# A four-layer mixer trunk: the convolution layers' output projection taken block by block, and the first layer's norm of block 1 beside its first tile

## The chip, the cores and the metric

The kernel runs on one core of a Trainium2 chip. The metric is device time in microseconds of one execution; the profile comes from one further execution that the hardware profiler recorded.

## What is computed

One step of a hybrid trunk over 128 context and 1024 latent tokens of width 1024, four layers. Layers 0 and 3 are widened Conformer convolutions, layer 1 is gated neighbourhood attention, layer 2 a gated bidirectional scan. Each layer is a modulated RMSNorm, a mixer and a gated residual; a final RMSNorm follows. The convolution mixer is the part that matters here:

```python
def modulated_norm(x, cond, ada_w, ada_b, norm_w):
    mod = jax.nn.silu(cond) @ ada_w + ada_b
    shift, scale, gate = jnp.split(mod[:, None, :], 3, axis=-1)
    h = rms_norm(x, norm_w) * (1 + scale) + shift
    return h, gate

def conformer_conv_mixer(h, w_in, b_in, w_dw, b_dw, ln_w, ln_b, w_out, b_out):
    v, g, z = jnp.split(h @ w_in + b_in, 3, axis=-1)
    u = v * jax.nn.sigmoid(g)
    u = depthwise_conv(u, w_dw, b_dw)
    u = jax.nn.silu(layer_norm(u, ln_w, ln_b))
    return (u * jax.nn.silu(z)) @ w_out + b_out
```

## The kernel before

The 1152 tokens are three blocks (b0, b1, b2) of 384 columns; the width is eight tiles of 128 partitions. Every product with a weight is made in three passes of split numbers: `unit` (L466) runs, for each of eight k, `wh·hh` (L471), `wh·hl` (L472) and `wl·hh` (L473), 24 matmuls for one output tile of one block. Weight tiles come by DMA from SP's queue into `raw`, and `wsplit` (L432, L433) makes `wh` on ACT and `wl` on `w_eng`, which is GpSimd (POOL) but in layer 2; `wh` and `wl` have two buffers each, and one weight ahead is split when a weight is taken.

The order of the work is the order in which the program issues it, engine by engine. After each unit `tick` runs some of the work that stands in lists: up to four `steps` (the convolution's taps among them) and three advances (`GENS_A_UNIT`) of the first generator in `gens`, which holds norms. A norm is such a generator. `rstd` and `rstd_row` issue the sum over partitions, `st_ps` (L303 or L314; the latter after ACT has copied `row`, L312), and the twelve small VectorE operations `nr_a`, `nr_y`, `nr_z` of `rsqrt` (L323 to L331), called the chain below; `spread` then yields LAG = 4 times and issues `dg` (L340, VectorE), the matmul `rs_ps` (L344) that spreads the row, and `rstd` (L346, ACT). After that the norm issues per k `nt` (L360, VectorE), `hh` (L363, ACT) and `hl` (L364, VectorE), or in the convolution's LayerNorm `conv_norm` (L705): `mu` (L716, ACT), c − mu (L720, VectorE for even k, POOL for odd), its square (L722, ACT), the sum `var` (L723, PE), then the chain, then the scaling (L731, VectorE), silu (L733, ACT), the product with the gate path z, which is read back from DRAM (L734, VectorE), `gh` (L735, ACT) and `gl` (L736, POOL).

`start` runs 16 conditioning tiles (`ada_tile`, L244, L253) and norm 0 of block 0 among them, then block 1's, then hands block 2's to `gens`. `conv_layer` (L603) then loops over eight tiles of the width: the units of g and v of all three blocks, and the depthwise convolution `dwconv` of the tile, whose taps run on VectorE (L775), ACT and POOL beside the next tile's units. The last tile's taps of blocks 1 and 2 (`rest`), the LayerNorms and the units of z's last tile fill what follows. `out_proj` (L576) then projects: the first weights (m = 0, 1) for b0 and b1, m = 2 to 7 each for b0 and b1, and then all eight again for b2. `out_unit` adds the residual (`xm`, read from DRAM; L557, L566) and the sum of squares (L292 to L296), and `next_norm` hands the next layer's norm of a finished block to `gens`. In layer 3 a transposed final norm follows each unit instead (L1515, L1517).

Of the kernel before, what the change touches and what calls it, by code (L numbers as in the profile page):

```python
# [9 lines left out]
F32 = mybir.dt.float32  # L10
# [9 lines left out]
P = 128  # L20
D = 1024
KT = D // P
# [49 lines left out]
TAIL = {0: TAIL0, 3: TAIL3}  # L72


REST = 4
# [5 lines left out]
VAR_MM = 2  # L81

# [78 lines left out]
def run(steps):  # L161
    for s in steps:
        s()
        yield
# [10 lines left out]
class Kern:  # L175
    def __init__(self, ctx, tc, A, O, depth):
        self.tc, self.nc, self.A, self.O = tc, tc.nc, A, O
        nc = self.nc
        self.const = ctx.enter_context(tc.tile_pool(name="const", bufs=1))
        self.blkp = ctx.enter_context(tc.tile_pool(name="blk", bufs=9))  # L180
        self.wraw = ctx.enter_context(tc.tile_pool(name="wraw", bufs=3))
        self.wsp = ctx.enter_context(tc.tile_pool(name="wsp", bufs=2))
        self.work = ctx.enter_context(tc.tile_pool(name="work", bufs=2))
        self.dram = ctx.enter_context(tc.tile_pool(name="dram", bufs=1, space=DRAM))
        self.mmp = ctx.enter_context(tc.tile_pool(name="mm", bufs=3, space=PSUM))
        self.xs = [A["x"]] + [self.dram.tile([P, KT, T], F32, name=f"xs{i}") for i in range(1, DEPTH)]
        self.pend, self.steps, self.trickle, self.gens, self.slow = [], [], [], [], []
        self.raws, self.split, self.wi = {}, {}, 0
        self.w_eng = nc.gpsimd
        self.h = [None] * NB  # L190
        self.ada_end = lambda: None
        self.depth = depth
        self.specs = self.weight_specs()
# [177 lines left out]
    def weight_specs(self):  # L371
# [5 lines left out]
        for l in range(self.depth):  # L377
# [27 lines left out]
                        for i in SSD_ADA[b][m]:  # L405
                            ada(l + 1, i)
            if kind != 2:
                out += [(w[m], P) for g in range(2) for m in range(KT)]
        return out

    def wload(self, i, pool=None):
# [12 lines left out]
    def wsplit(self, i):  # L424
        if i < len(self.specs) and i not in self.split:
            nc = self.nc
            self.wload(i)
            width, raw = self.specs[i][1], self.raws.pop(i)
            wh = self.wsp.tile([P, KT, P], F32R, name="wh", tag="wh")
            wl = self.wsp.tile([P, KT, P], F32R, name="wl", tag="wl")  # L430
            s = raw[:, :, :width]
            nc.scalar.copy(out=wh[:, :, :width], in_=s)  # L432
            self.w_eng.tensor_tensor(out=wl[:, :, :width], in0=s, in1=wh[:, :, :width].bitcast(F32),  # L433
                                     op=ALU.subtract)
            self.split[i] = wh, wl

# [43 lines left out]
    def tick(self):  # L480
        for _ in range(STEPS_A_UNIT):
            if not self.steps:
                break
            self.steps.pop(0)()
        for _ in range(GENS_A_UNIT):
            self.advance()
        if self.slow and next(self.slow[0], StopIteration) is StopIteration:
            self.slow.pop(0)
        for _ in range(2):
            if self.trickle:  # L490
                self.trickle.pop(0)()
        due, self.pend = self.pend, []
        for e in due:
            e[0] -= 1
        for e in due:
            if e[0] <= 0:
                e[1]()
        self.pend = [e for e in due if e[0] > 0] + self.pend
# [77 lines left out]
    def out_proj(self, l, g, bias=None, order=None):  # L576
        nc = self.nc
        with self.tc.tile_pool(name="xm", bufs=2, reuse_waits="tile") as pool:
            self.out_begin(l, bias, pool)
            for grp in ((0, 1), (2,)):  # L580
                x0, x1 = (grp[0] * BW, (grp[-1] + 1) * BW) if order is None else (0, T)
                for ms in [(0, 1)] + [(m,) for m in range(2, KT)]:
                    w, xm = {}, {}
                    for m in ms:
                        w[m] = self.wtake()
                        xm[m] = pool.tile([P, x1 - x0], F32, name="xm", tag="xm", bufs=2)
# [16 lines left out]

    def conv_layer(self, l, j, order):
        nc, tc, h = self.nc, self.tc, self.h
        with tc.tile_pool(name="cp", bufs=1, space=PSUM, reuse_waits="tile") as cp, ExitStack() as stack:
            cw = stack.enter_context(tc.tile_pool(name="cw", bufs=2, reuse_waits="tile"))
            close = stack.close
# [75 lines left out]
            due, self.pend = self.pend, []  # L684
            for e in due:
                e[1]()
            self.lz = cw
            rest = run(chain(*rest))
            lns[0] = also(lns[0], rest, REST)
            z, nz = chain(*[z_tile(m) for m in TAIL[l][1]]), NB * len(TAIL[l][1])  # L690
            interleave(part(z, TAIL[l][2]), TAIL[l][2], part(lns[0], 9), 9)
            for _ in rest:
                pass
            lns[0] = also(lns[0], part(lns[1], 9))
            interleave(part(lns[0], TAIL[l][3]), TAIL[l][3], z, nz - TAIL[l][2])
            self.flush()
            close()
            with tc.tile_pool(name="lz", bufs=3, reuse_waits="tile") as self.lz:
                for _ in lns[0]:
                    pass  # L700
                self.gens += lns[1:]
                self.out_proj(l, g, bias=("conv_b_out", j * KT), order=order)

    def conv_norm(self, cp, b, j, c, s1, sums, zd, g):

        nc = self.nc
        if b == VAR_MM:
            self.var = cp.tile([P, 3 * 512], F32, name="var", tag="ca", bufs=1)
        if b < 2:
            sums(KT - 1, (b,))  # L710
        else:
# [6 lines left out]
        var = self.var[:, 512 * b:512 * b + BW] if b >= VAR_MM else self.mm("var")[:, :BW]  # L718
# [6 lines left out]
        r = yield from self.rstd_row(var, D, LN_EPS)  # L725
        gh, gl = self.blk(f"gh{b}", F32R), self.blk(f"gl{b}", F32R)
        for k in range(KT):
            z = self.lz.tile([P, BW], F32, name="zk", tag="zk", bufs=3)
# [4 lines left out]
            nc.scalar.activation(out=ck, in_=ck, func=AF.Silu, bias=self.v("conv_ln_b", j * KT + k))  # L733
            nc.vector.tensor_tensor(out=ck, in0=ck, in1=z, op=ALU.mult)  # L734
            nc.scalar.copy(out=gh[:, k, :], in_=ck)  # L735
            nc.gpsimd.tensor_tensor(out=gl[:, k, :], in0=ck, in1=gh[:, k, :].bitcast(F32), op=ALU.subtract)  # L736
            yield
        g[b] = gh, gl

# [797 lines left out]
    def start(self, pool):  # L1537
# [31 lines left out]
        for k in range(KT):  # L1569
# [2 lines left out]
                if RAW0 + 2 * k + i < 2 * KT:  # L1572
                    load(RAW0 + 2 * k + i)
            if k == NORM_0:
                steps(0, 1 + LAG + k)
            elif k > NORM_0:
                steps(0, 1)
            if k == TURN_1:
# [3 lines left out]
        self.ada_end()  # L1582
        steps(0, 9)
        self.wsplit(2 * KT + 1)
        steps(1, 1 + LAG + 9)
        self.x_sums(2)
        self.gens.append(self.norm(0, 2, self.xb[2], self.acc[2], self.h))

# [92 lines left out]
```

## Time and profile before

| | |
|---|---|
| median of 3 executions | 2966.41 us (2965.76 to 2966.68) |
| profiled execution | 2963.28 us, its span 2961.5 us |
| mean granted PE clock | 0.975 |
| PE busy | 2789.2 us (94%), 17561 matmuls |
| VectorE (DVE), ACT, POOL busy | 69%, 42%, 45% |
| layer 0's convolution loop | to about 400 us |
| layer 0's projection ends | 582.3 us |
| layer 3's projection ends | 2948.7 us |

How to read it: the profiled execution took 1.8 us more than its span, and stands 3.1 us under the median. A matmul of 384 columns starts about 0.17 us after the one before it at full clock, and its record is longer than that, since matmuls overlap. fp32 matmuls (`var`, `st_ps`, `rs_ps`) leave two records each. Idle time in front of an instruction stands behind it in brackets, with what ended it.

### The profile page before, as it was taken

The page shows a single profiled execution, that of the slowest core. Times are in us where ns is not written, and L with a number is a line of the kernel's source. Part 1 is how long each engine was busy: PE and PEld are TensorE (multiplying, and loading weights), DVE is VectorE, ACT ScalarE, POOL GpSimd, SP SyncE. Part 2 cuts the span into 40 slices and gives each one's busy share as a digit, 9 for nine tenths or more (in the row PEclk, how much of TensorE's full clock was granted, in tenths as well). Part 3 has the DMA queues.
Part 4 walks back from the last instruction along what each step waited for, and adds up shares of the span by engine and source line. Part 5 has one row for each costly group of instructions (what it writes and reads, how often), then busy time and mean ns, then how long its engine had stood idle before and what let it go on. Part 6 is the DMA issues. An engine that isn't in the chain of part 4 may idle for free. (4 is left out here: it accounts for less than half of the span.)

```text
span 2961.5 us, 45878 instructions
## 1 busy us (share of the span) xinstructions
PE 2789.2 (94%) x17561; PEld 2527.8 (85%) x17561; DVE 2047.6 (69%) x3319; ACT 1249.9 (42%) x2188; POOL 1347.5 (45%) x800
## 2 busy tenths in 40 slices
PE   5999988899999999999999999998899999999888
PEld 4999967889999998888999998877667889999678
DVE  5899886553554445537887778977986565999963
ACT  4455455443333333444443333222323444555553
POOL 4688766611001110244114443634644346888755
PEclk8999999999999999999999999999999999999989
DMA  5232324632222233335235559876886752111134
GB/s 220 65 121 97 102 82 146 226 105 83 73 84 85 88 91 90 120 116 188 87 105 173 167 177 325 304 219 210 253 288 223 254 179 93 54 59 58 63 119 141
DMA packets 231547, 424.45 MB, mean 143 GB/s; under 512 B 19552, under 2 KB 149408, under 8 KB 231328
## 3 DMA queue, kind: packets, MB, share of 16 engines
q1 hardware_dynamic: 229280, 417.50, 43.9%
q10 hardware_dynamic: 2048, 4.02, 0.4%
q8 instruction: 139, 2.28, 0.3%
q14 instruction: 80, 0.66, 0.1%
HBM read 331.83 MB, written 79.66 MB: 139 GB/s over the span
## 5 line engine op out<-in xcount | busy, mean ns | idle before, releaser
L433 POOL TENSOR_TENSOR wl<-raw,wh 128x1024 fp32r<-128x1024 f32 x169 | 407.8, 2414 | 960.0 <-ACT wh L432 916.7
L775 DVE SCALAR_TENSOR_TENSOR ca<-u,vec,ca 128x1167 f32<-128x1167 f32 (+4 forms) x420 | 481.5, 1146 | 11.3
L768 POOL TENSOR_TENSOR pa<-pa,pt 128x1167 f32<-128x1167 f32 (+4 forms) x189 | 399.6, 2116 | 78.1 <-ACT pa L763 37.0
L432 ACT CAST wh<-raw 128x1024 fp32r<-128x1024 f32 (+1 forms) x239 | 249.4, 1044 | 404.9 <-PE op L472 89.6
L471 PE MATMUL in_ps<-hh,wh 128*128 128x384 f32 x768 | 268.4, 352 | 3.9 <-DVE nt L866 2.7
L472 PE MATMUL in_ps<-hl,wh 128*128 128x384 f32 x768 | 262.5, 342 | 0.7 <-DVE hl L364 0.7
L473 PE MATMUL in_ps<-hh,wl 128*128 128x384 f32 x768 | 262.0, 341 | 0.0
L767 ACT ACTIVATE pt<-u,vec 128x1167 f32<-128x1167 f32 (+4 forms) x189 | 194.1, 1039 | 126.0 <-POOL pa L768 124.6
L471 PE MATMUL op<-gh,wh 128*128 128x384 f32 x576 | 201.8, 351 | 14.7 <-ACT gh L735 8.8
L473 PE MATMUL op<-gh,wl 128*128 128x384 f32 x576 | 199.8, 348 | 12.5 <-POOL wl L433 12.5
L1289 DVE SCALAR_TENSOR_TENSOR sca<-ub,vec,sca 128x1155 f32<-128x1155 f32 x144 | 205.0, 1423 | 3.5
L471 PE MATMUL x_ps<-hh,wh 128*128 128x384 f32 x576 | 203.2, 353 | 1.4 <-ACT ub L1240 0.7
L472 PE MATMUL op<-gl,wh 128*128 128x384 f32 x576 | 201.4, 350 | 0.8 <-POOL gl L736 0.8
L473 PE MATMUL x_ps<-hh,wl 128*128 128x384 f32 x576 | 196.0, 341 | 0.0
L472 PE MATMUL x_ps<-hl,wh 128*128 128x384 f32 x576 | 195.9, 340 | 0.0
L471 PEld LDWEIGHTS in_ps<-hh,wh 128*128 128x128 f32 x768 | 145.4, 189 | 13.6 <-issue 7.0
L296 POOL TENSOR_TENSOR ssq<-ssq,sq 128x384 f32<-128x384 f32 x105 | 110.5, 1054 | 86.4 <-ACT sq L295 85.2
L472 PEld LDWEIGHTS in_ps<-hl,wh 128*128 128x128 f32 x768 | 145.6, 190 | 3.2 <-DVE hl L364 1.5
L473 PEld LDWEIGHTS in_ps<-hh,wl 128*128 128x128 f32 x768 | 145.5, 190 | 3.1 <-issue 2.4
L471 PE MATMUL op<-sgh,wh 128*128 128x384 f32 x384 | 135.1, 352 | 6.5 <-DVE xm L566 2.5
L473 PE MATMUL sz_ps<-hh,wl 128*128 128x384 f32 x384 | 139.3, 363 | 0.0
L473 PE MATMUL op<-sgh,wl 128*128 128x384 f32 x384 | 133.5, 348 | 4.9 <-POOL wl L433 4.3
(281 smaller groups left out, 7605.0 us busy)
## 6 DMA issues: line engine op xcount, KB each, us to landing
raw<-in_ada_w SPq DMA_DIRECT2D x96, 512.0 KB, 4.6
rw<-ssd_rows SPq DMA_DIRECT2D x72, 512.0 KB, 5.7
raw<-in_ssd_w_in SPq DMA_DIRECT2D x62, 512.0 KB, 4.3
raw<-in_conv_w_in SPq DMA_DIRECT2D x48, 512.0 KB, 3.5
raw<-in_ssd_w_out SPq DMA_DIRECT2D x48, 512.0 KB, 4.4
raw<-in_conv_w_out SPq DMA_DIRECT2D x32, 512.0 KB, 3.6
raw<-in_na_w_in SPq DMA_DIRECT2D x32, 512.0 KB, 3.5
ssd_xtok<-xtk SPq DMA_DIRECT2D x20, 576.0 KB, 3.5
```

Of the source, the lines that this page charges most:

```text
L296: nc.gpsimd.tensor_tensor(out=acc, in0=acc, in1=sq, op=ALU.add)
L432: nc.scalar.copy(out=wh[:, :, :width], in_=s)
L433: self.w_eng.tensor_tensor(out=wl[:, :, :width], in0=s, in1=wh[:, :, :width].bitcast(F32), op=ALU.subtract)
L471: nc.tensor.matmul(out, lhsT=wh[:, k, :width], rhs=hh[:, k, :], start=f, stop=False)
L472: nc.tensor.matmul(out, lhsT=wh[:, k, :width], rhs=hl[:, k, :], start=False, stop=False)
L473: nc.tensor.matmul(out, lhsT=wl[:, k, :width], rhs=hh[:, k, :], start=False, stop=l)
L767: nc.scalar.activation(out=pt, in_=u_t, func=AF.Copy, scale=wt(t))
L768: nc.gpsimd.tensor_tensor(out=p, in0=p, in1=pt, op=ALU.add)
L775: nc.vector.scalar_tensor_tensor(out=c, in0=u_t, scalar=wt(t), in1=c, op0=ALU.mult, op1=ALU.add)
L1289: nc.vector.scalar_tensor_tensor(out=ca, in0=u[:, t:t + SCLEN], scalar=wt(t), in1=ca, op0=ALU.mult, op1=ALU.add)
```

## The change

Three things are done.

First, at the start, `rs_ps` of block 0 is issued after two more conditioning tiles, and block 1's norm is put into `gens`, so that it advances behind the first tile's units, which come as `hh` of block 0 does.

Second, in both convolution layers the last taps of block 1 go beside the LayerNorm of block 0 (two in each step), those of block 2 beside the LayerNorm of block 1, and the LayerNorms of blocks 1 and 2 go into `gens`, beside the projection. The projection goes block by block, eight output tiles each, so each weight tile is loaded and split three times instead of twice and serves one unit. While it runs, `tick` makes five advances instead of three, and every third `wl` is made by VectorE. z is read back into slices of a convolution buffer, `xm` shares the buffers of `sg`, and the sums `var` of blocks 1 and 2 have banks of their own.

Third, `gl` of even k is made on VectorE, that of odd k on POOL.

```diff
@@ tick @@
-        for _ in range(GENS_A_UNIT):
+        for _ in range(self.rate):
             self.advance()
@@ weight tiles @@
-                out += [(w[m], P) for g in range(2) for m in range(KT)]
+                out += [(w[m], P) for g in range(NB if kind == 0 else 2) for m in range(KT)]
@@ wsplit @@
-            self.w_eng.tensor_tensor(out=wl[:, :, :width], in0=s, in1=wh[:, :, :width].bitcast(F32),
+            eng = self.w_eng[i % len(self.w_eng)] if isinstance(self.w_eng, list) else self.w_eng
+            eng.tensor_tensor(out=wl[:, :, :width], in0=s, in1=wh[:, :, :width].bitcast(F32),
                                      op=ALU.subtract)
@@ out_proj @@
-            for grp in ((0, 1), (2,)):
+            grps = ((0,), (1,), (2,)) if pool else ((0, 1), (2,))
+            for grp in grps:
...
-                for ms in [(0, 1)] + [(m,) for m in range(2, KT)]:
+                for ms in [(0, 1)] + [(m,) for m in range(2, KT)] if len(grps) == 2 else [(m,) for m in range(KT)]:
@@ conv_layer @@
-            self.lz = cw
-            rest = run(chain(*rest))
-            lns[0] = also(lns[0], rest, REST)
-            z, nz = chain(*[z_tile(m) for m in TAIL[l][1]]), NB * len(TAIL[l][1])
-            interleave(part(z, TAIL[l][2]), TAIL[l][2], part(lns[0], 9), 9)
-            for _ in rest:
+            self.zk = [up[KT % 3][:, i * BW:(i + 1) * BW] for i in range(3)]
+            rest = [run(r) for r in rest]
+            ln0 = also(lns[0], rest[0], REST)
+            z = chain(*[z_tile(m) for m in TAIL[l][1]])
+            interleave(part(ln0, 9), 9, part(z, 1), 1)
+            interleave(part(ln0, 1 + LAG), 1 + LAG, z, 2)
+            for _ in ln0:
                 pass
-            lns[0] = also(lns[0], part(lns[1], 9))
-            interleave(part(lns[0], TAIL[l][3]), TAIL[l][3], z, nz - TAIL[l][2])
             self.flush()
-            close()
-            with tc.tile_pool(name="lz", bufs=3, reuse_waits="tile") as self.lz:
-                for _ in lns[0]:
-                    pass
-                self.gens += lns[1:]
-                self.out_proj(l, g, bias=("conv_b_out", j * KT), order=order)
+            self.gens += [chain(rest[0], also(lns[1], rest[1], 2), rest[1], lns[2])]
+            self.rate, self.w_eng = RATE_TAIL, [nc.gpsimd, nc.vector, nc.gpsimd]
+            self.out_proj(l, g, bias=("conv_b_out", j * KT), order=order, pool=cw)
+            self.rate, self.w_eng = GENS_A_UNIT, nc.gpsimd
@@ conv_norm @@
-            nc.gpsimd.tensor_tensor(out=gl[:, k, :], in0=ck, in1=gh[:, k, :].bitcast(F32), op=ALU.subtract)
+            (nc.gpsimd if k % 2 else nc.vector).tensor_tensor(out=gl[:, k, :], in0=ck, in1=gh[:, k, :].bitcast(F32),
+                                                              op=ALU.subtract)
@@ start @@
             if k == NORM_0:
-                steps(0, 1 + LAG + k)
+                steps(0, 1)
+            elif k == NORM_0 + 1:
+                steps(0, LAG + k)
...
-        steps(1, 1 + LAG + 9)
+        self.gens.append(norms[1])
```

`REST` is 2 instead of 4, and the new `RATE_TAIL` is 5.

The order on three places. First PE at the start, before, from block 0's sum on (`ada_ps` are the conditioning tiles, `g_ps` the first units):

```order
L303 MATMUL st_ps<-ones,ssq_125 128x1 x3
L344 MATMUL rs_ps<-dg,ones 128x384
L244 MATMUL ada_ps<-raw_192,sc 32x128 x8
...
L253 MATMUL ada_ps_501<-sel,ada_sb 128x2
L303 MATMUL st_ps<-ones,ssq_245 128x1 x3
L344 MATMUL rs_ps<-dg,ones 128x384
L471 MATMUL g_ps<-hh_359,wh 128x384
```

And in the change:

```order
L304 MATMUL st_ps<-ones,ssq_125 128x1 x3
L245 MATMUL ada_ps<-raw_192,sc 32x128 x8
L254 MATMUL ada_ps_362<-sel,ada_sb 128x2
L245 MATMUL ada_ps<-raw_208,sc 32x128 x8
L254 MATMUL ada_ps_377<-sel,ada_sb 128x2
L345 MATMUL rs_ps<-dg,ones 128x384
...
L254 MATMUL ada_ps_501<-sel,ada_sb 128x2
L473 MATMUL g_ps<-hh_388,wh 128x384
```

Block 0's `rs_ps` has moved behind two conditioning tiles, and the first unit stands directly behind the last of them; block 1's `st_ps` now stands in the middle of that unit and its `rs_ps` behind block 0's two units.

Second, PE in layer 0's projection, at the LayerNorm of block 2, before (`op` are the projection's units; a unit's three lines repeat eight times between the two sums' matmuls):

```order
L723 MATMUL var<-sq,ones 128x384
L473 MATMUL op<-gh_4119,wl 128x384
L314 MATMUL st_ps<-ones,row 128x1 x3
L471 MATMUL op<-gh_3901,wh 128x384
L472 MATMUL op<-gl_3902,wh 128x384
...
L473 MATMUL op<-gh_3901,wl 128x384
L344 MATMUL rs_ps<-dg,ones 128x384
```

In the change, at the same LayerNorm and then at the next layer's norm of block 0:

```order
L475 MATMUL op<-gh_3852,wl 128x384
L726 MATMUL var<-sq,ones 128x384 x7
L315 MATMUL st_ps<-ones,row 128x1 x3
L345 MATMUL rs_ps<-dg,ones 128x384
L473 MATMUL op<-gh_3852,wh 128x384
...
L304 MATMUL st_ps<-ones,ssq_3923 128x1 x3
L345 MATMUL rs_ps<-dg,ones 128x384
L473 MATMUL op<-gh_4135,wh 128x384
```

Where 24 matmuls stood between sum and spread, none stands now; the same holds at the norm of block 1, and in layer 3 at the LayerNorm of block 2.

Third, VectorE at the next layer's norm of block 0 in the change (the chain's steps are the `nr_` rows, L737 is the product with z):

```order
L435 TENSOR_TENSOR wl<-raw,wh 128x1024
L739 TENSOR_TENSOR gl_4431<-c_841,gh_4430 128x384
L568 SCALAR_TENSOR_TENSOR xr_4523<-op,mod_98,nt 128x384
L324 TENSOR_SCALAR nr_a<-st_ps 128x3
L737 TENSOR_TENSOR c_841<-c_841,u_548 128x384
L325 TENSOR_SCALAR nr_y<-nr_a 128x3
L737 TENSOR_TENSOR c_841<-c_841,u_548 128x384
L327 TENSOR_SCALAR nr_y<-nr_y 128x3
L739 TENSOR_TENSOR gl_4431<-c_841,gh_4430 128x384
L330 SCALAR_TENSOR_TENSOR nr_z<-nr_y,nr_a 128x3
...
L341 TENSOR_TENSOR dg<-ident,nr_y 128x384
```

Two products with z and one `gl` of block 2, and a `wl` just ahead, now stand among the first steps of the chain; the last one of the twelve is followed at once by `dg`.

## Rows read from the trace of the kernel before

**Rows 1.** Stretches: us busy (x instructions) per engine, PE clock, DMA share, GB/s

```profile
core 0: us, PE busy (x) PEld busy (x) DVE busy (x) ACT busy (x) POOL busy (x), PEclk, DMA share, GB/s
...
100.00:400.00 300.00, 297.60 (x2087) 283.72 (x2085) 268.51 (x297) 165.05 (x210) 240.40 (x111) 1.00 0.32 104
400.00:500.00 100.00, 78.50 (x333) 61.81 (x334) 75.48 (x128) 50.46 (x103) 57.87 (x46) 0.90 0.34 114
...
2800.00:2900.00 100.00, 85.15 (x435) 75.81 (x434) 65.87 (x118) 54.05 (x107) 60.80 (x46) 0.90 0.40 123
```

**Rows 2.** Waits of PE: us in total, times, longest us

```profile
PE rs_ps L344 <- DVE dg L340: 23.6, 8, 7.8
...
PE op L473 <- POOL wl L433: 16.8, 13, 2.1
```

**Rows 3.** Timeline of PE, start: start us, us, engine, line, operation [idle <-releaser]

```profile
33.12 1.62 PE L344 MATMUL rs_ps<-dg,ones 128*128 128x384 f32 x2 [3.11 <-DVE dg L340]
...
62.84 1.62 PE L344 MATMUL rs_ps<-dg,ones 128*128 128x384 f32 x2 [7.81 <-DVE dg L340]
...
70.75 0.42 PE L471 MATMUL v_ps<-hh,wh 128*128 128x384 f32 x1
...
74.83 0.34 PE L473 MATMUL v_ps<-hh,wl 128*128 128x384 f32 x1
```

**Rows 4.** Timeline of VectorE, start

```profile
57.19 0.48 DVE L364 SCALAR_TENSOR_TENSOR hl<-nt,mod,hh 128x256 fp32r<-128x256 f32 x1
...
75.92 0.61 DVE L364 SCALAR_TENSOR_TENSOR hl<-nt,mod,hh 128x384 fp32r<-128x384 f32 x1
...
98.04 1.44 DVE L773 TENSOR_SCALAR ca<-u,vec 128x1167 f32<-128x1167 f32 x1
```

**Rows 5.** Timeline of ACT, split of the second tile

```profile
93.16 1.05 ACT L432 CAST wh<-raw 128x1024 fp32r<-128x1024 f32 x1 [3.82 <-PE g_ps L472]
```

**Rows 6.** Timeline of PE, layer 0's tail and the next layer's start

```profile
453.40 1.32 PE L344 MATMUL rs_ps<-dg,ones 128*128 128x384 f32 x2 [2.69 <-DVE dg L340]
...
454.85 0.52 PE L473 MATMUL op<-gh,wl 128*128 128x384 f32 x1
...
455.81 0.52 PE L473 MATMUL op<-gh,wl 128*128 128x384 f32 x1
...
459.39 0.34 PE L473 MATMUL op<-gh,wl 128*128 128x384 f32 x1
...
466.38 1.33 PE L471 MATMUL op<-gh,wh 128*128 128x384 f32 x2 [6.66 <-ACT gh L735]
...
582.00 0.34 PE L473 MATMUL op<-gh,wl 128*128 128x384 f32 x1
...
590.90 0.66 PE L471 MATMUL in_ps<-hh,wh 128*128 128x384 f32 x1 [2.71 <-DVE nt L866]
```

**Rows 7.** Timeline of VectorE, row-norm chain of block 1, first and last step

```profile
447.35 0.15 DVE L323 TENSOR_SCALAR nr_a<-st_ps 128x3 f32<-128x3 f32 x1
...
452.70 0.56 DVE L340 TENSOR_TENSOR dg<-ident,nr_y 128x384 f32<-128x384 f32 x1
```

**Rows 8.** Timeline of VectorE, then of POOL, scalings and c − mu

```profile
455.29 8.15 DVE L731 SCALAR_TENSOR_TENSOR c<-c,vec,rstd 128x384 f32<-128x384 f32 x8 [1.10 <-ACT rstd L346]
463.36 0.55 DVE L720 TENSOR_TENSOR c<-c,mu 128x384 f32<-128x384 f32 x1
...
456.29 5.15 POOL L720 TENSOR_TENSOR c<-c,mu 128x384 f32<-128x384 f32 x4
```

**Rows 9.** Timeline of PE, layer 3's tail

```profile
2822.32 0.34 PE L473 MATMUL op<-gh,wl 128*128 128x384 f32 x1
...
2833.77 2.93 PE L723 MATMUL var<-sq,ones 128*128 128x384 f32 x4 [9.94 <-ACT sq L722]
...
2948.35 0.34 PE L473 MATMUL op<-gh,wl 128*128 128x384 f32 x1
```

**Rows 10.** Line 433: engine, duration ns min/median/max, first and last start us

```profile
L433 POOL TENSOR_TENSOR wl<-raw,wh x169: 1277/2398/3594, 35.4 to 2940.7; 128x1024 fp32r<-128x1024 f32 x168, 128x512 fp32r<-128x512 f32 x1
L433 DVE TENSOR_TENSOR wl<-raw,wh x70: 1203/1226/2817, 1758.4 to 2380.1; 128x1024 fp32r<-128x1024 f32 x70
```

More of the change, by code (lines that the diff above doesn't have):

```diff
@@ L72 @@
 TAIL = {0: TAIL0, 3: TAIL3}
-REST = 4
+REST = 2
+RATE_TAIL = 5
 VECS = [("c", KT), ("c_ctx", KT), ("ada_b", 24 * DEPTH), ("norm_w", KT * DEPTH), ("conv_b_in", 48), ("conv_b_dw", 16),
@@ L80 @@
 VEC0 = sum(n for _, n in VECS[:4])
-VAR_MM = 2
 NA_FIRST = (0, 1), (2,), (3,)
@@ L189, in __init__ @@
         self.w_eng = nc.gpsimd
+        self.rate = GENS_A_UNIT
         self.h = [None] * NB
@@ L574, in out_unit, with out_proj @@
             nc.sync.dma_start(out=self.xs[l + 1][:, :, b * BW:(b + 1) * BW], in_=self.xb[b])
-    def out_proj(self, l, g, bias=None, order=None):
+    def out_proj(self, l, g, bias=None, order=None, pool=None):
         nc = self.nc
-        with self.tc.tile_pool(name="xm", bufs=2, reuse_waits="tile") as pool:
+        with ExitStack() as stack:
+            grps = ((0,), (1,), (2,)) if pool else ((0, 1), (2,))
+            pool = pool or stack.enter_context(self.tc.tile_pool(name="xm", bufs=2, reuse_waits="tile"))
             self.out_begin(l, bias, pool)
-            for grp in ((0, 1), (2,)):
+            for grp in grps:
                 x0, x1 = (grp[0] * BW, (grp[-1] + 1) * BW) if order is None else (0, T)
-                for ms in [(0, 1)] + [(m,) for m in range(2, KT)]:
+                for ms in [(0, 1)] + [(m,) for m in range(2, KT)] if len(grps) == 2 else [(m,) for m in range(KT)]:
                     w, xm = {}, {}
@@ L585, in out_proj @@
                         w[m] = self.wtake()
-                        xm[m] = pool.tile([P, x1 - x0], F32, name="xm", tag="xm", bufs=2)
+                        n, tag = (T, "sg") if len(grps) == 3 else (x1 - x0, "xm")
+                        xm[m] = pool.tile([P, n], F32, name="xm", tag=tag, bufs=2)[:, :x1 - x0]
                         nc.sync.dma_start(out=xm[m], in_=self.xs[l][:, m, x0:x1])
@@ L605, in conv_layer @@
         nc, tc, h = self.nc, self.tc, self.h
-        with tc.tile_pool(name="cp", bufs=1, space=PSUM, reuse_waits="tile") as cp, ExitStack() as stack:
-            cw = stack.enter_context(tc.tile_pool(name="cw", bufs=2, reuse_waits="tile"))
-            close = stack.close
+        with tc.tile_pool(name="cp", bufs=1, space=PSUM, reuse_waits="tile") as cp, \
+                tc.tile_pool(name="cw", bufs=2, reuse_waits="tile") as cw:
             up = [cw.tile([P, ULEN], F32, name=f"u{i}", bufs=1) for i in range(3)]
@@ L686, in conv_layer @@
                 e[1]()
-            self.lz = cw
-            rest = run(chain(*rest))
-            lns[0] = also(lns[0], rest, REST)
-            z, nz = chain(*[z_tile(m) for m in TAIL[l][1]]), NB * len(TAIL[l][1])
-            interleave(part(z, TAIL[l][2]), TAIL[l][2], part(lns[0], 9), 9)
-            for _ in rest:
-                pass
-            lns[0] = also(lns[0], part(lns[1], 9))
-            interleave(part(lns[0], TAIL[l][3]), TAIL[l][3], z, nz - TAIL[l][2])
+            self.zk = [up[KT % 3][:, i * BW:(i + 1) * BW] for i in range(3)]
[5 more added lines that the diff above has]
+            for _ in ln0:
+                pass
             self.flush()
-            close()
-            with tc.tile_pool(name="lz", bufs=3, reuse_waits="tile") as self.lz:
-                for _ in lns[0]:
-                    pass
-                self.gens += lns[1:]
-                self.out_proj(l, g, bias=("conv_b_out", j * KT), order=order)
+            self.gens += [chain(rest[0], also(lns[1], rest[1], 2), rest[1], lns[2])]
+            self.rate, self.w_eng = RATE_TAIL, [nc.gpsimd, nc.vector, nc.gpsimd]
+            self.out_proj(l, g, bias=("conv_b_out", j * KT), order=order, pool=cw)
+            self.rate, self.w_eng = GENS_A_UNIT, nc.gpsimd
     def conv_norm(self, cp, b, j, c, s1, sums, zd, g):
         nc = self.nc
-        if b == VAR_MM:
-            self.var = cp.tile([P, 3 * 512], F32, name="var", tag="ca", bufs=1)
         if b < 2:
@@ L717, in conv_norm @@
         yield
-        var = self.var[:, 512 * b:512 * b + BW] if b >= VAR_MM else self.mm("var")[:, :BW]
+        if b == 0:
+            var = self.mm("var")[:, :BW]
+        else:
+            shape, tag, bufs = ([P, 512], "s1", 2) if b == 1 else ([P, 3 * 512], "ca", 1)
+            var = cp.tile(shape, F32, name="var", tag=tag, bufs=bufs)[:, :BW]
         for k in range(KT):
@@ L727, in conv_norm @@
         for k in range(KT):
-            z = self.lz.tile([P, BW], F32, name="zk", tag="zk", bufs=3)
+            z = self.zk[k % 3]
             nc.sync.dma_start(out=z, in_=zd[:, k, b * BW:(b + 1) * BW])
```

## The prediction

> **What bounds the kernel now.** I read the stretches of the span first, then the list of waits, then the timelines of the places that the change touches. The stretch 100 to 400 us shows TensorE (PE) busy 297.60 of 300 us at granted clock 1.00 [rows 1]: in the main loop only PE's own work counts, so a time won ahead of it moves everything after it, and none can be won in it. The stretches 400 to 500 and 2800 to 2900 are different: PE is busy 78.50 and 85.15 of 100 us at a granted clock of 0.90, a mean of the two levels 1.2 and 2.4 GHz [rows 1]. They are the tails of the two convolution layers. The list of waits names what is missing: rs_ps waits for VectorE's dg eight times, 23.6 us in all, and the third product of a unit waits for GpSimd's wl thirteen times, 16.8 us [rows 2]. PE takes its instructions in order, so each of these waits holds back all that stands behind it.
>
> **The measure.** One unit is 24 matmuls: 70.75 to the end of the one at 74.83, 4.2 us [rows 3]. The profiled execution took 2963.28 us, 3.13 under the median of 2966.41; the sum is made against the former and 3.13 added at the end. About 0.2%, 5.9 us, is what a measurement of this kernel can tell from no change.
>
> **Part 1, the start.** rs_ps of block 0 waits 3.11 us for the row-norm chain on VectorE; then rs_ps of block 1 waits 7.81, to 62.84, and only after it does the first unit run [rows 3]. In the change two conditioning tiles stand between st_ps and rs_ps of block 0, which covers most of the 3.11, and block 0's first unit no longer stands behind block 1's norm. Block 0's hl is ready at 57.67 (the row at 57.19 and its 0.48) [rows 4], so its two units can be done near 62 instead of at the end of the row at 74.83, 75.2 [rows 3]. That is not 13 us of gain: VectorE must still make block 1's and block 2's inputs, block 1's to 76.53 (the row at 75.92) [rows 4], and that stream starts with the same rs_ps and moves forward by 1 to 3 us only. What is won is that block 1's and 2's units run as their inputs come instead of one unit behind them: the convolution's first tap, now at 98.04 [rows 4], moves to about 91, 7 us. Part of it goes back. Both weights of the first tile are now freed together, by block 2's last matmuls, so the next tile's split is no longer hidden: ACT's wh takes 1.05 us [rows 5] and POOL's wl 2.40 [rows 10], of which I leave 2.5 us uncovered. **Term −4.5**, bounds −7 (split hidden) and −3 (all of it and some delay of rs_ps bare). Since the main loop is full, this reaches the end.
>
> **Part 2, the front of layer 0's tail.** Before, the two units of block 0 end at 459.73 (the row at 459.39) and the next waits 6.66 us, to 466.38, for block 1's gh [rows 6]. In the change block 0 goes on to its third output tile, and asks only for a new weight; but st_ps of block 1's LayerNorm stands ahead of that unit and needs its eight squares first. Half of the last taps have left the first LayerNorm, which brings block 0's two units to about 457.5; the squares hold the third to about 462.8. **Term −3.6**, bounds −6.7 (the whole wait) and 0.
>
> **Part 3, layer 0 from there to its end.** From 466.38 to 582.34 (the row at 582.00) [rows 6] are 116 us. 22 units of 4.2 are 92, the LayerNorm's and the norms' small matmuls about 9; 15 are waits and low clock. The work stays the same. What changes is where it waits. With five generator steps to a unit, more than the four that a row norm leaves between its sum and its spread, st_ps and rs_ps fall into one step, and the order shows them adjacent three times: at block 2's LayerNorm, and at the next layer's norms of blocks 0 and 1. Before, 24 matmuls or more stood between. Now PE stands still for the whole chain. Alone that costs what the start shows, 3.11 us [rows 3]. Beside work of POOL the same chain takes from 447.35 to 453.26 (the row at 452.70), 5.9 us [rows 7], and where VectorE's products stand between its steps, more.
>
> The three, in turn. At block 2's LayerNorm the squares stand in ACT's order behind block 1's last gh, and c − mu on VectorE behind eight scalings of block 1, which beside POOL take 8.15 us; eight like the single product at 463.36 would take 4.4 [rows 8]. Block 1's gh come to about 492; PE has done its first seven output tiles by 487; eight squares, the sum, the chain: about 503, less 6 us of small matmuls in between, **10**. At the next layer's block 0 two products c·z, each waiting for ACT's silu, and a gl stand between the chain's steps on VectorE: 7 to 11, I take **9**. At block 1 one wl of 1.2 us [rows 10] stands in it: about **6.5**, near the 5.9. After such a wait the clock is low: behind the 2.69 us at 453.40, three matmuls take 0.96 us (454.85 to 455.81) [rows 6], 0.32 each against 0.17, and nine of them are like that, **1.5** per wait. Now each weight serves one unit, not two, in two passes of three: I put **5** on waits for wl, of the kind that cost 1.3 each [rows 2] (four of them; ends 3 and 10). 10 + 9 + 6.5 + 4.5 + 5 = 35 against 15: **term +19.9**. Lower end: three times 3.1, the same 4.5 and 3 make 16.8, **+1.7**; upper end 11 + 11 + 6.5 + 4.5 + 10 = 43, +28.
>
> One thing in it is a matter of ports. While POOL's c − mu run (4 in 5.15 us), VectorE's products with two inputs come about one to each of them [rows 8]. The Trainium skill, page "SBUF — State Buffer", section "Who interferes with whom", says that such a VectorE instruction and a reading GpSimd instruction exclude each other for their whole length; the trace agrees: eight times 0.55 and four times some 1.0 are 8.4, against the 8.15 measured. By that rule, handing a third of wl and half of gl to VectorE shortens no stretch in which both are busy; my sum already takes none of it as a gain.
>
> **Part 4, the next layer.** Its first unit waits 2.71 us for block 1's and 0's inputs now [rows 6]; with both norms done beside the projection that goes. **Term −2.7**, upper end 0.
>
> **Part 5, layer 3's tail.** The same edit without the next layer's norms: the final norm has no such pair in the order. Block 1's sums wait 9.94 us for ACT's squares, to 2833.77 [rows 9], behind two units that end at 2822.66 (the row at 2822.32). From there to 2948.69 (the row at 2948.35) [rows 9] are 126 us: 22 units of some 4.4 (the final norm's transposes stand in them) are 97, small matmuls 8.5, waits and low clock 20.5. The change starts its third unit near 2828.8, 6.1 after the second, by the same reckoning as in part 2; then come one in-order chain of 10 with its 1.5 of clock, and 3 for weights: 20.6. **Term +0.1**, bounds −6 (the chain at 3.1 to 4) and +5. What follows the last unit stays the same.
>
> The added DMAs (eight weight tiles and eight residual tiles per layer) are asked for two units ahead and cost nothing while they land within 4 us; the wait list has no transfer of that kind.
>
> **Sum.** −4.5 − 3.6 + 19.9 − 2.7 + 0.1 = +9.2: 2963.28 + 9.2 + 3.13 = 2975.6 us, slower by 0.3%.
>
> **Rivals.** (A) The four chains stay cheap: VectorE reaches the twelve small steps while POOL is idle, because POOL has a third less wl and half the gl, and each adjacent pair costs the 3.1 us of the start. Then part 3 is +1.7 and part 5 −6: −15.1, 2951. It decides when the four average less than about 6.6 us (10 + 9 + 6.5 + 10 is 35.5; less 9.2, by four). For it: the uncontended row; against it: the 5.9 us of [rows 7], beside POOL. (B) They average between about 5.1 and 8.1: gains and losses meet, about 2966. (C) The weights bind: one unit of 4.2 us has to cover wh 1.05 and wl 2.40 on engines that take other work in between; if one unit in three waits 1.3 us, both tails lose 10 instead of 5 and 3, 12 more, and the time is about 2987. For it: the thirteen waits; against it: a third of the splits moves to VectorE at 1.23 us [rows 10]. (D) The new start gains nothing, since the main loop is held by VectorE's taps: against it the 297.60 us; then 2980.
>
> **Chances.** Forecast (slower, some 2972 to 2983, D in it) 0.38, C 0.12, B 0.20, A 0.30. So faster by over 0.2% 0.30, within 0.20, slower 0.50. The range takes in A's centre and C's: 2950 to 2987; the forecast's own is 2972 to 2983.
>
> **What would show it.** The first tap on VectorE near 91 us; PE's rs_ps waiting for dg in four new places of 6 to 11 us, the total of that wait rising from 23.6 to about 40; the waits of 6.66 and 9.94 gone; the last unit of layer 0 some 9 us later than now. I am wrong if those rs_ps waits are near 3 us, if PE waits for wl at nearly every unit, or if the next layer starts earlier than now.

## The result, and the profile after

The changed kernel takes 2989.27 us (median of 4, 2987.62 to 2996.44) against 2966.09 before: ratio 1.009, 95% interval 1.0065 to 1.0115. It is slower, as forecast, but by 23 us and not by 9, and outside the range, which ended at 2987. The profiled execution of the changed kernel took 2990.64 us with a span of 2988.9, so its trace holds 27.4 us more than that of before. Cut at the same landmarks in both traces (the last product of the convolution's loop, the start of the projection's third unit, the projection's end), they lie here (the forecast of a row is the term of the prediction that belongs to it):

| stretch | before | change | difference | forecast |
|---|---|---|---|---|
| to the end of layer 0's loop | 397.26 | 389.17 | −8.1 | −4.5 |
| from there to the third unit | 69.1 | 64.9 | −4.3 | −3.6 |
| third unit to the end of layer 0's projection | 116.0 | 151.8 | +35.8 | +19.9 |
| from there to the end of layer 3's loop | 2185.4 | 2178.8 | −6.6 | −2.7 |
| layer 3's tail to its last unit | 181.0 | 191.5 | +10.5 | +0.1 |

The first fence shows the change's start, on PE and then on VectorE.

```profile
33.34 1.65 PE L345 MATMUL rs_ps<-dg,ones 128*128 128x384 f32 x2 [0.30 <-DVE dg L341]
...
44.93 0.67 PE L473 MATMUL g_ps<-hh,wh 128*128 128x384 f32 x1
...
89.41 1.43 DVE L777 TENSOR_SCALAR ca<-u,vec 128x1167 f32<-128x1167 f32 x1
```

Where [rows 3] had waits of 3.11 and 7.81 us ahead of the first unit, block 0's rs_ps now waits 0.30, and the first unit starts at 44.93 instead of 63.68. The first tap on VectorE is at 89.41 instead of 98.04 [rows 4]. The next fence is the change's stretches (the columns of [rows 1]); the two long ones run to the last unit, in layer 0 from the start of the third unit, in layer 3 from the end of the second.

```profile
100.00:400.00 300.00, 296.13 (x2073) 281.08 (x2071) 269.69 (x298) 163.56 (x215) 239.05 (x113) 1.00 0.33 109
400.00:500.00 100.00, 72.92 (x300) 55.11 (x298) 74.15 (x135) 52.55 (x102) 49.60 (x36) 0.85 0.42 140
...
2800.00:2900.00 100.00, 73.97 (x332) 60.97 (x331) 79.52 (x147) 54.59 (x104) 45.63 (x34) 0.83 0.32 101
...
454.00:605.80 151.80, 117.21 (x574) 106.36 (x574) 103.37 (x178) 75.68 (x137) 74.67 (x45) 0.88 0.54 187
...
2838.70:2976.10 137.40, 119.82 (x651) 111.92 (x650) 82.45 (x156) 68.44 (x118) 71.82 (x46) 0.93 0.44 143
```

And the same two of the kernel before:

```profile
466.40:582.30 115.90, 106.65 (x567) 100.61 (x568) 63.63 (x124) 60.92 (x117) 73.62 (x50) 0.97 0.56 185
...
2822.70:2948.70 126.00, 112.96 (x634) 105.53 (x633) 65.83 (x130) 61.18 (x111) 77.96 (x54) 0.95 0.39 123
```

Read these two pairs as idle time and as clock. In layer 0 PE is idle 34.6 us instead of 9.3 (151.80 less 117.21; 115.90 less 106.65), 25 more; and for the same products it is busy 10.6 us longer, with a granted clock of 0.88 instead of 0.97. In layer 3 it is 4.5 us more of idle time and 6.9 more of busy time, but about 4 of these 6.9 are work that stood ahead of the stretch before (24 records of `var` fall into it instead of 16, and a `st_ps`), so some 3 are left for the clock. VectorE has 103 us of work in layer 0's stretch instead of 64: block 1's and 2's LayerNorms and the next norms now run beside the projection.

The waits of PE in the change (us in total, times, longest), against [rows 2]:

```profile
PE rs_ps L345 <- DVE dg L341: 31.3, 9, 9.8
PE var L726 <- ACT sq L725: 28.1, 7, 8.9
PE op L475 <- POOL wl L435: 13.9, 9, 2.1
...
PE yps L1519 <- DVE fx L568: 9.2, 2, 8.7
```

The wait for dg is 13 us less at the start and 20 us more in the tails. The timeline of PE in layer 0 shows a new wait ahead of the projection and then the three adjacent pairs:

```profile
430.57 1.65 PE L726 MATMUL var<-sq,ones 128*128 128x384 f32 x2 [8.95 <-ACT sq L725]
...
454.04 0.44 PE L473 MATMUL op<-gh,wh 128*128 128x384 f32 x1
...
488.15 1.65 PE L726 MATMUL var<-sq,ones 128*128 128x384 f32 x2 [4.43 <-ACT sq L725]
...
500.27 1.62 PE L345 MATMUL rs_ps<-dg,ones 128*128 128x384 f32 x2 [3.49 <-DVE dg L341]
...
515.70 0.72 PE L304 MATMUL st_ps<-ones,ssq 128*128 128x1 f32 x6
526.24 1.65 PE L345 MATMUL rs_ps<-dg,ones 128*128 128x384 f32 x2 [9.81 <-DVE dg L341]
...
528.01 0.52 PE L474 MATMUL op<-gl,wh 128*128 128x384 f32 x1
...
531.85 0.52 PE L474 MATMUL op<-gl,wh 128*128 128x384 f32 x1
...
567.32 0.72 PE L304 MATMUL st_ps<-ones,ssq 128*128 128x1 f32 x6
572.98 1.65 PE L345 MATMUL rs_ps<-dg,ones 128*128 128x384 f32 x2 [4.93 <-DVE dg L341]
```

The waits of 6.66 and 9.94 us [rows 6, rows 9] are gone, but PE now waits 8.95 us for block 1's first square ahead of the projection's first unit (430.57), and in layer 3 the same 8.95 at 2820.06. At 515.70 and 526.24 sum and spread stand one behind the other, with 9.81 us of nothing between them. After it, twelve matmuls from 528.01 to 531.85 take 0.32 us each, the lower of the two levels (1.2 against 2.4 GHz), and the whole unit, 527.12 to 534.1, takes 7.0 us instead of 4.3. What VectorE did in those 9.81 us:

```profile
519.09 0.14 DVE L324 TENSOR_SCALAR nr_a<-st_ps 128x3 f32<-128x3 f32 x1
519.15 2.10 DVE L737 TENSOR_TENSOR c<-c,u 128x384 f32<-128x384 f32 x1
521.18 0.96 DVE L325 TENSOR_SCALAR nr_y<-nr_a 128x3 int32<-128x3 int32 x1
522.05 0.55 DVE L737 TENSOR_TENSOR c<-c,u 128x384 f32<-128x384 f32 x1
...
523.24 0.99 DVE L331 TENSOR_TENSOR nr_z<-nr_z,nr_y 128x3 f32<-128x3 f32 x1
...
525.63 0.56 DVE L341 TENSOR_TENSOR dg<-ident,nr_y 128x384 f32<-128x384 f32 x1
```

And GpSimd beside it:

```profile
518.30 2.53 POOL L435 TENSOR_TENSOR wl<-raw,wh 128x1024 fp32r<-128x1024 f32 x1
520.80 1.31 POOL L297 TENSOR_TENSOR ssq<-ssq,sq 128x384 f32<-128x384 f32 x1
523.22 0.99 POOL L739 TENSOR_TENSOR gl<-c,gh 128x384 fp32r<-128x384 f32 x1 [1.11 <-ACT gh L738]
```

The sum was ready at 516.4; its first step waited to 519.09, behind a wl, a gl and a result of the projection. A product with z then took 2.10 us while GpSimd made a wl, and two steps of the chain that take 0.15 us alone took 0.96 and 0.99: each ended with the GpSimd operation beside it (522.1 and 524.2). Layer 3 has one wait that no order of PE could show:

```profile
2850.75 9.76 DVE L734 SCALAR_TENSOR_TENSOR c<-c,vec,rstd 128x384 f32<-128x384 f32 x8
2860.43 1.95 DVE L723 TENSOR_TENSOR c<-c,mu 128x384 f32<-128x384 f32 x4
2862.31 3.63 DVE L737 TENSOR_TENSOR c<-c,u 128x384 f32<-128x384 f32 x3
2865.86 0.73 DVE L568 SCALAR_TENSOR_TENSOR fx<-op,mod,nt 128x128 f32<-128x128 f32 x2
```

The unit whose result is read at 2865.86 had ended at 2858.0. Fifteen operations of the LayerNorms of blocks 1 and 2 stood ahead of it in VectorE's queue, and PE waited 8.73 us for fx. This also corrects a sentence ahead of the prediction: the order on an engine is not quite the program's. Each generator step issues one scaling, yet eight stand in a row, so the order in an engine's queue is settled when the program is compiled.

### The profile page after: what moved, and what is told of

Read it like the earlier page. It is cut to its first block, busy times and chain, and to the rows that moved or that the text cites. A ratio compares the mean times of both kernels' runs of the same rounds, so it can differ in the third digit from the quotient of the medians.

```text
span 2988.9 us, 45991 instructions
## 1 busy us (share of the span) xinstructions
PE 2799.6 (94%) x17561; PEld 2538.1 (85%) x17561; DVE 2082.7 (70%) x3359; ACT 1267.4 (42%) x2204; POOL 1332.5 (45%) x776
## 5 line engine op out<-in xcount | busy, mean ns | idle before, releaser
L433 ACT CAST wh<-raw 128x1024 fp32r<-128x1024 f32 (+1 forms) x255 | 266.2, 1044 | 414.2 <-issue 85.6
L297 POOL TENSOR_TENSOR ssq<-ssq,sq 128x384 f32<-128x384 f32 x105 | 117.7, 1122 | 94.6 <-ACT sq L296 86.9
L435 DVE TENSOR_TENSOR wl<-raw,wh 128x1024 fp32r<-128x1024 f32 x86 | 119.0, 1384 | 35.6 <-ACT wh L433 35.5
```

The source lines that it names most:

```text
L297: nc.gpsimd.tensor_tensor(out=acc, in0=acc, in1=sq, op=ALU.add)
```

## The experiments

**Which part does what.** The start alone, on the kernel before (the two edits of `start` in the diff, nothing else):

> The kernel before with the first part of the change alone (the start). In the two traces the convolution's main loop of layer 0 ends 8.1 us earlier with the change (389.2 against 397.3 us). Theory: the start's gain is real and stands by itself, so this kernel takes about 2966 - 8 = 2958 us. Rival: the tail of layer 0 gives it back, because what it waits for is set by other engines: 2964 to 2967.

Measured: 2953.39 us against 2962.22 for the kernel before beside it, ratio 0.9984 (0.9971 to 0.9997); the ratio is not that of the two medians, which lie further apart. In its trace the loop ends at 389.33 us and layer 0's projection at 575.3 instead of 582.3, so layer 0's tail does not give the gain back. The tails alone, that is the change with `start` as before:

> The change with its start undone: only the tails are changed. Theory: start and tails add up, so about 2989 + 8 = 2997 us. Rival: the two overlap, 2989.

Measured: 2992.31 us, ratio 1.0101 (1.0073 to 1.0128), between the theory and its rival; the interval takes in both. The start is a gain by itself and all of the loss is in the tails. By its interval the start is worth 1 to 9 us; the 8.1 us of the trace lie within that, and so does less.

This run also says how far a single trace can be trusted, since behind the start its program is that of the change. From the third unit to the end of layer 0's projection it has

```profile
459.90:609.70 149.80, 114.98 (x573) 104.18 (x573) 103.48 (x178) 75.86 (x137) 73.99 (x45) 0.89 0.54 189
```

that is 149.8 us instead of 151.8, with the same idle time (34.8) and 8.3 us of longer matmuls instead of 10.6. From there to the end of layer 3's loop it takes 2186.5 us where the change took 2178.8.

**The adjacent pairs.**

```
-        for _ in range(LAG):
+        for _ in range(LAG if self.rate == GENS_A_UNIT else 9):
             yield
```

> The change, but while the projection runs a row norm leaves nine generator steps between its sum and its spread instead of four, so that one unit of 24 matmuls stands between st_ps and rs_ps again. Theory 1, the adjacent pairs are what costs: of the four waits (3.5, 9.8 and 4.9 us in layer 0, 3.5 in layer 3) 4.2 us each are covered, 15 us, and 4 to 6 us of low clock behind them go too: 2968 to 2971. Rival, theory 2, the burst of five steps per unit on VectorE and ACT is what costs (the squares, and the projection's results queued behind eight scalings), and PE waits at the next thing instead: 2983 to 2990, with the 8.7 us wait for fx in layer 3 still there.

Measured: 2971.51 us, ratio 1.0035 (1.0018 to 1.0052): 18 us less than the change (16 by the ratios), half a microsecond above what theory 1 said. Its waits in layer 0, and its two long stretches:

```profile
478.30 0.66 PE L473 MATMUL op<-gh,wh 128*128 128x384 f32 x1 [6.25 <-DVE xr L568]
...
502.22 0.81 PE L345 MATMUL rs_ps<-dg,ones 128*128 128x384 f32 x2
...
531.10 1.65 PE L345 MATMUL rs_ps<-dg,ones 128*128 128x384 f32 x2 [6.72 <-DVE dg L341]
...
452.20:586.70 134.50, 111.96 (x573) 103.84 (x573) 106.25 (x178) 74.37 (x134) 69.37 (x43) 0.92 0.61 207
2819.60:2957.10 137.50, 120.75 (x650) 112.48 (x649) 82.33 (x156) 68.09 (x118) 73.01 (x46) 0.93 0.43 143
```

The wait at block 2's spread is gone (502.22 has none), that at the next layer's block 0 is still 6.72, and a new one of 6.25 for a result stands ahead. Layer 0 from the third unit is 134.5 us instead of 151.8, so 15 to 17 us of the 34 to 36 hung on the pairs. Layer 3 gained nothing (137.5 for 137.4), and there theory 2 was right: its one pair was replaced by other waits.

Three steps per unit (`RATE_TAIL = 3`), which part the pairs and thin the bursts:

> The change with three generator steps per unit in the projection, as before, instead of five. This separates sum and spread by a unit and also thins the bursts on VectorE and ACT. Theory 1: the same as with nine steps between, 2968 to 2971. Theory 2: the waits for squares (10.6 us at block 2's LayerNorm with its chain, in layer 0), for fx (8.7) and the low clock behind them go as well: 2950 to 2960, clearly under the nine-step kernel. Rival, theory 3: the LayerNorms come too late for the blocks that need them, and PE waits for gh of blocks 1 and 2: 2985 or more.

Measured: 2977.64 us, ratio 1.0061 (1.0041 to 1.0081). By the medians 12 us better than the change, though the two intervals overlap, and not better than the nine-step kernel; theory 2's numbers are missed by some 18 us at least. PE waits 9.4 us for dg at the next layer's norm of block 0, about as long as in the change.

**VectorE's queue.** The order edge (what a unit's steps issue on VectorE stands behind the reading of that unit's result), with nine steps between sum and spread, and then with the pairs adjacent:

```
+            last = nc.vector.scalar_tensor_tensor(out=xo[:, s0:s1], in0=ps[:, s0:s1], ...)
+        if self.rate != GENS_A_UNIT:
+            with self.tc.issue_after(last.ins):
+                self.tick()
```

> The kernel with nine steps between sum and spread, and besides, on VectorE, what a unit's generator steps issue stands behind the reading of that unit's result (an order edge; no instruction is added or left out). In the nine-step kernel PE still waits 8.4 us for xr and 13.5 for fx over both tails, because scalings that the LayerNorm issues stand ahead of the results in VectorE's queue. Theory 2: these 22 us go, some of it turns into other waits: 2952 to 2962. Rival: the LayerNorm now gets through VectorE later, and PE waits for its squares, dg and gh instead: 2968 to 2980.

> The change with only that order edge, and sum and spread adjacent as in the change. Theory 1 (adjacent pairs): their four waits stay, only the 8.7 us for fx and the 3.3 for a bank in layer 3 go: 2977 to 2981. Rival: the chain to dg now stands behind a result too, so the adjacent pairs get longer: 2989 or more.

Measured: 3004.5 us (ratio 1.0146) and 3001.13 (1.0137). Both theories missed. The second rival holds, the first in kind alone: the nine-step kernel lost 33 us, and 3004.5 lies far above its 2980. The waits for fx went (from 13.9 us to 0.4 against the nine-step kernel) and those for dg grew (from 15.9 to 25.8). But the compiled order of the other engines moved with the edges: the projection's first unit came 12 to 14 us earlier on PE and waited 9.7 and 8.9 us for gh in the two tails, where the kernels without the edge wait 8.95 for a square. So this is no clean test of one queue, and what the 33 us are made of was not settled. That the LayerNorms are as urgent as the results they stand ahead of is how I read it; it is not shown.

**Who does the splits.** The change with wl and gl all on GpSimd (`w_eng` a list of `nc.gpsimd` alone, `gl` as before):

> The change with all of wl and gl on GpSimd, as before. It takes about 8 splits of 1.2 us and 12 products of 0.55 to 1.4 us per layer off VectorE. Theory 2 (VectorE's queue is what PE waits for): the 9.8 us chain at the next layer's block 0 and the 8.7 us wait for fx shrink, 2975 to 2983 us. Rival (the weights bind): GpSimd has to give a wl of 2.4 us for every unit of 4.2 and eight gl besides, and the 9 us of waits for wl and wh in layer 0 double: 2992 to 3000.

Measured: 3007.07 us, ratio 1.0161 (1.0139 to 1.0183), 18 us slower than the change. The number fits the rival, its reason doesn't:

```profile
PE rs_ps L345 <- DVE dg L341: 39.2, 9, 11.7
PE var L726 <- ACT sq L725: 27.7, 13, 8.9
PE op L475 <- POOL wl L435: 15.5, 11, 2.1
PE yps L1519 <- DVE fx L568: 13.1, 3, 7.7
```

The wait for GpSimd's wl rose by 1.6 us, against 2.1 of waits for VectorE's wl that went (3.3 to 1.2); those for dg, fx and the projection's results rose by 8, 4 and 6. VectorE had less to do and was later. A wl takes GpSimd 2.40 us and VectorE 1.23 [rows 10], a gl 1.0 to 1.3 and 0.55. A reading that fits, though no run tests it by itself: where the two exclude each other, a split given to GpSimd costs VectorE more time than doing it itself.

**The clock.** Matmuls of constants between sum and spread of the four adjacent pairs, with nothing shortened:

```
+        with self.tc.issue_after(st.ins):
+            for _ in range(n):
+                self.nc.tensor.matmul(ps[:, :P], lhsT=self.ones, rhs=self.ident, start=True, stop=True)
```

> The change with matmuls of constants, whose results nobody reads, put between the sum and the spread of the four adjacent pairs (14 at block 2's LayerNorm in both layers, 20 at the next layer's blocks 0 and 1): PE does something in these waits, no wait is shortened. From the third unit of layer 0's projection to its end PE is busy 117.2 us with the change and 106.7 before, for the same matmuls; in layer 3 119.8 and 113.0. Theory (low clock behind the stops is most of what the prediction left out): the units behind the four pairs take 4.4 us again instead of 5.9 to 7.0, and rs_ps 0.8 instead of 1.6; the time falls by 5 to 10 us against the change, 2979 to 2984. Rival: the clock stays low all the same, or other stops (squares, weights) bring it down: 2988 to 2992.

Measured: 2984.0 us, ratio 1.007 (1.0049 to 1.009), by the medians 5 us less than the change; the two intervals overlap, so the time alone does not show a gain. The units do. The three pairs of layer 0:

```profile
494.54 3.39 PE L315 MATMUL fill<-ident,ones 128*128 128x128 f32 x28
498.10 0.88 PE L357 MATMUL rs_ps<-dg,ones 128*128 128x384 f32 x2 [0.17 <-DVE dg L353]
...
512.42 4.73 PE L315 MATMUL fill<-ident,ones 128*128 128x128 f32 x40 [0.17 <-DVE xr L580]
521.87 1.13 PE L357 MATMUL rs_ps<-dg,ones 128*128 128x384 f32 x2 [4.72 <-DVE dg L353]
...
564.76 4.71 PE L315 MATMUL fill<-ident,ones 128*128 128x128 f32 x40
569.84 0.91 PE L357 MATMUL rs_ps<-dg,ones 128*128 128x384 f32 x2 [0.37 <-DVE dg L353]
```

Where the fill left 0.17 and 0.37 us of idle time, rs_ps took 0.9 us instead of 1.6 and the unit behind it 4.6 instead of 6.4 and 5.9; where 4.72 us were left, the unit took 6.2. In layer 3 it is the same: 0.16 us left, rs_ps 0.9, and the unit 4.4 instead of 6.0. The low clock is what follows a stop of PE, and it is a price of its own beside the wait. The stretch from the third unit to layer 0's end is 147.0 us, against 151.8 and 149.8 in the two traces without the fill.

**A version that beats both.** The start and the division of work, with the old order of projection and LayerNorms:

> The kernel before with the start of the change and with the change's division of work (every third wl of the convolution's projections and gl of even k on VectorE), but the old order of the projection and of the LayerNorms. In the change that division is worth 15 to 18 us (without it 3007 us). Theory: it helps wherever GpSimd is late, and before it is: 6.7 and 2.0 us of waits for wl in the two tails. Then 3 to 8 us under the kernel with the start alone, 0.993 to 0.996 of the kernel before. Rival: VectorE is as scarce there as GpSimd, they exclude each other, and nothing is won: 0.998 to 1.001, or worse where a dg or c - mu is later.

> As the kernel before with the start and the division of work, but with gl all on GpSimd: only every third wl of the convolution's projections goes to VectorE. Theory: the gain is in wl, since PE waits for wl and hardly for gl (0.8 us): the same as with both, 0.993 to 0.996. Rival: gl counts, because POOL's gl stand ahead of its c - mu and wl: half of the gain or none.

> The kernel before with the start of the change and gl of even k on VectorE, every wl on GpSimd. With both parts of the division it was 0.993 of the kernel before, with wl alone 0.9965, about what the start alone gives (0.998). Theory: gl is the part that pays, because GpSimd's eight gl of a block, 1.0 to 1.3 us each, stand ahead of its c - mu of the next block: 0.992 to 0.995. Rival: it takes both, gl alone puts VectorE's scalings and squares later: 0.996 to 0.999.

Measured: 2944.9 us, ratio 0.9929 (0.9909 to 0.995), with both; 0.9965 (0.9953 to 0.9977) with wl alone; 0.9953 (0.9936 to 0.997) with gl alone; the start alone was 0.9984. With both parts the division is a gain of some 0.5% beside the start, clear of noise, and the first theory holds. The single parts come out at 0.2 and 0.3%, which add up to that; wl alone is not clear of the start alone, since their intervals overlap, and gl alone is just clear. For wl alone the rival holds (half of the gain or none), for gl alone the number lies between theory and rival. In the waits of the version with both, wl is down from [rows 2]:

```profile
PE rs_ps L344 <- DVE dg L340: 10.5, 5, 5.0
...
PE op L474 <- POOL wl L434: 9.9, 7, 2.1
...
PE yps L1518 <- DVE fx L567: 8.6, 3, 6.5
```

Most of the fall of the first line is the start's (12.7 us with the start alone). The wait for wl was 16.4 with the start alone; against that fall of 6.5 stands a wait for fx of 8.6 where there was 0.6. So the list does not say where the gain is made, and that stays open.

## Why the prediction was wrong

**Right:** the direction, and the place of the loss. The start's parts came as described (first tap near 91 forecast, 89.41 measured); it was worth 8.1 and not 4.5 in the trace: of the 2.5 us charged for the next tile's split only 1.0 was seen (waits of 0.61 for wh and 0.38 for wl), and the tap came 8.6 us earlier instead of 7, since block 1's inputs on VectorE moved forward by 5.9 us (76.53 to 70.68) and not by 1 to 3. The front's number came as forecast, −4.3 for −3.6, but not its course: the 8.95 us for block 1's first square, ahead of the first unit, was not foreseen. The adjacent pairs are where they were expected, and in layer 0 their sizes are near: block 2's squares, sum and chain 10.6 us (1.55 + 4.43 + 0.61 + 0.56 + 3.49; forecast 10), the next norm's block 0 9.81 (forecast 9), block 1 4.93 (forecast 6.5). That the three add up to 25.4 for 25.5 is luck, since an error of −1.6 meets two of +0.6 and +0.8. The prediction's own sign, four waits of rs_ps for dg of 6 to 11 us and 40 in all, did not come: they are 3.49, 9.81, 4.93 and, in layer 3, 3.48, and 31.3 in all. At block 2's LayerNorm most of the 10.6 is the wait for ACT's squares, and the chain there and in layer 3 costs little more than the 3.11 of the start.

**Wrong, the term of part 3:** +19.9 was forecast and +35.8 came. The lost time in the change was forecast as 35 us: 25.5 of chains, 5 of weights, 4.5 of low clock. The first was met (25.4), the weights took 9.2, together the 34.6 us of idle time in the stretch. The rest is the clock. Before, by the prediction's reckoning, 15 us were lost, of which 9.3 were idle, so that 5.7 went to low clock; the change has 10.6 us of longer matmuls more than that (8.3 in the trace of the tails alone), so 16 us (14 there) and not 4.5. Of the 16 us that the term lacks, 12 are the clock and 4 the weights. The weights show a slip in the sum: before, this stretch already waits 8.2 us for wh and wl, and the change 9.2, so loading each weight oftener cost 1 us. The sum for the change put 5 for weights and 4.5 for clock where before 8.2 and, by the same reckoning, 5.7 were lost, and gave no reason why those should shrink. The failing step was "nine of them are like that, 1.5 per wait", read from behind a wait of 2.69 us. Behind waits of 3.5 to 9.8 us the next unit took 1.6 to 2.7 us more, rs_ps itself 0.8 more (which the row at 453.40 shows too, with its 1.32 us), and the sums between short waits for squares ran at the low clock too (at 490.40, four of them in 5.0 us, where one takes 0.8 at full clock). The fill confirms that it is the stop that costs: with no chain shortened, the unit behind it takes 4.6 us again.

**Wrong, the term of part 5:** +0.1 was forecast, +10.5 came. The term erred both ways. The chain cost 4.8 us (0.72 + 0.56 + 3.48) and not 10, and no weight was waited for where 3 us were put: some 8 us too much. What was not in the sum is the 8.73 us for fx: the prediction counted what PE waits for in its own order, and for VectorE only the chain; that a unit's result has to pass the same queue, behind eight scalings, was left out, and so were a wait of 3.26 us for a result bank whose reader stood in that queue, and most of the low clock: behind the three stops the units took 5.7, 6.0 and 6.0 us instead of 4.4, where one such price of 1.5 was put. A misreading changed nothing: the 9.94 us of before [rows 9] stand at the first sum of block 2's LayerNorm, not block 1's, whose eight sums are done before its st_ps at 2811.02.

**Not settled:** layers 1 to 3's loop, −6.6 for −2.7. The wait of 2.71 is gone, but the trace of the tails alone has +1.1 there (2186.5) with the same program, so the rest is no effect of the change that these traces could show.

**The rivals.** C (the weights bind) has the nearest number and the wrong reason: 9.2 us in layer 0 for 8.2 before, none in layer 3. A failed at its condition: the four cost 10.6, 9.8, 4.9 and, in layer 3, 4.8 us, 7.5 on average and not under 6.6, though its 3.1 was close at two of the four pairs (3.49 and 3.48). B's condition was met, between 5.1 and 8.1, and its time (about 2966) still did not come: the chains were near what was said, and the loss lay in the clock and in fx, which no rival had. D is out by the start alone. And the sentence that the division of work "shortens no stretch in which both are busy" did not lead to the right price. The Trainium skill, page "SBUF — State Buffer", section "Who interferes with whom", has the rule of exclusion, which the trace of the change bears out: a product of 0.55 us took 2.10 beside a wl of 2.53. What the prediction drew from it does not follow. The division is worth 18 us in the change, and together with the start it makes the fastest version; that work belongs on the engine that needs less time for it fits both, as a reading and not as something tested by itself.

What stays open: why the block-by-block order costs as much as it still does with the pairs parted. The nine-step kernel has the same start and division as the fastest version and takes 0.011 of the kernel before more, some 31 us; waits for xr, fx, dg and squares are spread over both tails, and neither the rate nor the order edge took the time away.

## What to carry to other kernels

When work is moved beside a busy engine, look in the new order for two dependent instructions that end up next to each other on an in-order engine: each such pair costs what is left of the chain between them, and on PE the low clock behind it as well, which is read from the busy time of the same instructions before and after, not from one example. Carry over into the sum for the new order every loss of the old one that nothing removes. Count in the other engine's queue everything that PE waits for, the reading of results included. And where VectorE and GpSimd exclude each other, compare the time that an operation takes on each, and try it on the faster one: here that gained 0.5%.

## What the runs showed that was not expected

A VectorE step of three columns, 0.15 us alone, takes 0.96 and 0.99 us beside GpSimd in the rows at 521.18 and 523.24, and 2.30 at 2428.16 in the same trace, beside a wl that ends with it; so a chain of twelve such steps is stretched by GpSimd operations that it meets. Taking 20 operations a convolution layer off VectorE made PE wait longer for VectorE, and the kernel took 18 us more. And constant matmuls in a wait, pure extra work, did not make the kernel slower: three of the four units behind them were faster by 1.3 to 1.8 us.
